# A two-layer token mixer with a mixture of experts: order of the last group's outputs, order of the first weight splits, and more expert weights on chip

## The chip, the cores and the metric

The kernel runs on one core of a Trainium2 chip. The core has a matrix engine (PE, with its weight loads shown as PEld), a vector engine (DVE), a scalar engine (ACT), a general engine (POOL) and an engine that mostly issues transfers (SP); sixteen DMA engines move data between the chip's large memory and the on-chip memory (SBUF). The metric is the device time of one execution in microseconds (us), lower is better. Before the change it is 1646.34 us, the median of three runs (1646.19 to 1651.53).

## The reference

The model has two layers on 256 tokens (`x`) and 256 context tokens (`ctx`), 1024 wide. In the last layer only the tokens go on, the context serves the mixers alone.

```
for each layer:
    mod = silu(c) @ w_mod + b_mod            # shifts, scales, gains; the same for the context
    h   = rms_norm(x) * (1 + scale) + shift
    p   = h @ w_in                           # inputs of four mixers and of their gates
    out = (sum of sigmoid(gate_i) * mixer_i(p)) @ w_mix_out     # s5, gla, window attention, conv
    x   = x + g1 * out
    x   = x + g2 * moe(rms_norm(x) * (1 + scale2) + shift2)
return rms_norm(x) * final_norm_g

moe(t):   # 4 groups of 8 experts
    the likeliest group of each token, the two best experts in it, their weights
    a = t @ w1[e];  b = t @ w3[e];  y += weight * (silu(a) * b) @ w2[e]
```

The weights of the 32 experts are 96 MB per layer, and all of them are read.

## The kernel before, in words

A planner (the tile framework) puts the instructions of each engine in order. It takes them as their data and buffers are free, earlier written ones first; instructions written under `high_priority` go ahead of all others that are ready. An explicit edge (`follow`) puts one instruction of an engine behind another. While `self.line` is a list, PE's instructions stay in the order in which they are written. Transfers of weights are all issued by SP, in one queue, in the planner's order; an issue whose buffer isn't free yet holds the queue.

**Layer start (`norm_h`, L539; `cm`, L623).** In layer 1 the two tiles of the tokens (t = 2, 3) are normed first, then those of the context (t = 0, 1): ACT squares and sums a tile, DVE makes a small value of the sum (`rnv`), POOL raises it to the power -1/2 (`rn`), and DVE (even t) or ACT (odd t) scales the tile to `xn`, which PE transposes. The first product after that, of the s5 input `u`, splits its weights into a high part (`wh`, ACT) and a low part (`wl`, DVE), in `split` under `high_priority`.

**Mix (`mix`, L1414).** Four quarters of `w_mix_out`. Each result bank is multiplied by the gain vector g1 (`prm`), which SP fetches from a scratch in the chip's memory (`vec`), and added to x. There are three result banks of this kind.

**Experts (`experts`, L1709).** The experts go in eight groups of four (`qd`). The weights of a group come in twelve quarters of 1 MB (`quarter`): j = 0 to 7 are w1 and w3 by blocks of 128 input rows, j = 8, 9 are w2's first column half, 10, 11 its second. `first` multiplies the gathered tokens by quarters 0 to 7 (`pab`), `hidden` makes silu(a) * b and transposes it, `second` multiplies by w2 (`pye`) and scales the result into `yy` (ACT the high part, DVE the low part), `combine` adds the scaled outputs into the tokens' rows with a 0/1 matrix (`pcb`), DVE multiplies by g2 (`pg`) and adds to x. The tokens of the next group are gathered by POOL (`fetch`, tile `xg`) and transposed (`pgt`).

Each group has 64 slots per expert in two blocks b of 32. In layer 0 (`PARTS` 1) both blocks serve all 512 rows. In layer 1 (`PARTS` 2, H = 2) block 0 holds slots of token tile 2 and block 1 those of tile 3.

Weights go to pools of 8 KB buffers: `wp`, used by the mixers too (three buffers in layer 0, four in layer 1), `mw` (six and nine), in layer 1 now and then the buffer of the context's x, no longer needed (`xp`, tag x0), and in layer 1 two quarters of the first group in `yy`, which later holds scaled outputs. `ahead` (L1869) names the quarters asked for before the experts start, nine and fourteen.

Tokens beyond the 64 slots of an expert are handled in a loop under a branch (`If`, L2013), not entered in these runs; in layer 0 one extra group of two experts (`x`) is computed always, beside group 6.

Of the kernel before, what the change touches and what calls it, by code (L numbers as in the profile page):

```python
# [19 lines left out]
D = 1024  # L20
# [157 lines left out]
class Net:  # L178
    def __init__(self, tc, A, out, dbg=None, stop=None):
        self.tc, self.nc, self.A, self.out = tc, tc.nc, A, out  # L180
        self.dbg, self.stop = dbg, stop
        self.line, self.behind = None, None
# [83 lines left out]
    def run(self):  # L266
        tc = self.tc
        with ExitStack() as cx:
# [11 lines left out]
            self.turns, self.spent = 0, False  # L280
# [10 lines left out]
    def consts(self):  # L291
# [9 lines left out]
        for n, sh in (("i16", [128, 16]), ("reset", [128, 512]), ("cos", [128, 256]), ("sin", [128, 256]),  # L301
                      ("rot", [128, 128]), ("mask", [128, 2, 128])):
            t = cp.tile(sh, F32, name="c_" + n)
            self.late.append((t, A[n]))
            self.cst[n] = t
# [27 lines left out]
    def slot(self, pool=None, sh=(128, 2048)):  # L333

        if pool is None:
            self.turns += 1
            if self.spent and self.turns % 4 == 0:
                return self.xp.tile(list(sh), F32, name="w", tag="x0")
        return (pool or self.wp).tile(list(sh), F32, name="w", tag="w")
# [75 lines left out]
    def vec(self, pool, l, name, s, tag="bc", **kw):  # L415

        b, q = {"g1": (0, 0), "sh2": (0, 2), "G2": (1, 0), "g2": (1, 2)}[name]
        t = pool.tile([128, D], F32, name=f"{name}{s}", tag=tag, **kw)
# [120 lines left out]
    def norm_h(self, l):  # L539

        sides = (0, 1) if l == 0 else (1, 0)
        with self.tc.tile_pool(name=f"nrm{l}", bufs=2, reuse_waits="tile") as np_:
# [15 lines left out]
            for s in sides:  # L558
                xn = []
                for t in (2 * s, 2 * s + 1):  # L560
# [8 lines left out]
                    else:  # L569
                        self.ts(xn[-1], xt, r, None, OP.mult)  # L570
# [52 lines left out]
    def cm(self, l, unit, t0, emit, blocks=(0, 1)):  # L623
# [827 lines left out]
    def moe_open(self, l):  # L1451
# [3 lines left out]
        self.spent = self.last  # L1455
# [9 lines left out]
        for n, sh in (("prio", [128, 44]), ("tok", [128, 4]), ("iota", [128, 512]), ("quad", [128, 4]),  # L1465
                      ("tri", [128, 128])):
            t = ro.tile(sh, F32, name="c_" + n)
            self.G.dma_start(t, self.A[n])
# [9 lines left out]
    def moe(self, l):  # L1478
# [6 lines left out]
        with ExitStack() as cx:  # L1485
# [3 lines left out]
            self.yy = cx.enter_context(tc.tile_pool(name=f"yy{l}", bufs=2 if self.last else 3, reuse_waits="tile"))  # L1489
            with tc.tile_pool(name=f"rl{l}", bufs=2, reuse_waits="tile") as tp:  # L1490
# [182 lines left out]
    def spread(self, pool, l, NT, R, tag):  # L1673
# [10 lines left out]
        t1 = new(NT, 32)  # L1684
# [24 lines left out]
    def experts(self, l, ep, R, more, later, hd, NT, NTOK, tiles):  # L1709
# [9 lines left out]
        g2 = {s: self.vec(ep, l, "g2", s, tag=f"g2{s}", bufs=1) for s in sorted({t // 2 for t in tiles})}  # L1719
# [148 lines left out]
        soon = [(0, 6), (0, 7)] if self.last else []  # L1868
# [266 lines left out]
```

## Time and profile before

| | |
|---|---|
| median of three runs | 1646.34 us |
| the profiled execution: its time | 1646.56 us |
| its span, first to last instruction | 1644.7 us |
| mean granted TensorE clock | 0.966 |
| PE busy | 1490.2 us, 91% |
| PEld busy | 962.2 us, 59% |
| DVE busy | 963.5 us, 59% |
| ACT busy | 534.4 us, 32% |
| POOL busy | 83.9 us, 5% |
| moved by DMA | 384.81 MB, mean 234 GB/s |

Layer 0's mix runs from about 590 to 637 us, its experts from 679 to 980; layer 1's mix from about 1331 to 1360, its experts from 1392 to 1634. A busy share is a mean over the span: what limits a stage is read from the engines and the DMA in that stage and from the waits there. A wait is put down to what came last.

### The profile page before, as it was taken

The page shows a single profiled execution, that of the slowest core. Times are in us where ns is not written, and L with a number is a line of the kernel's source. Part 1 is how long each engine was busy: PE and PEld are TensorE (multiplying, and loading weights), DVE is VectorE, ACT ScalarE, POOL GpSimd, SP SyncE. Part 2 cuts the span into 40 slices and gives each one's busy share as a digit, 9 for nine tenths or more (in the row PEclk, how much of TensorE's full clock was granted, in tenths as well). Part 3 has the DMA queues.
Part 4 walks back from the last instruction along what each step waited for, and adds up shares of the span by engine and source line. Part 5 has one row for each costly group of instructions (what it writes and reads, how often), then busy time and mean ns, then how long its engine had stood idle before and what let it go on. Part 6 is the DMA issues. An engine that isn't in the chain of part 4 may idle for free.

```text
span 1644.7 us, 26473 instructions
## 1 busy us (share of the span) xinstructions
PE 1490.2 (91%) x10595; PEld 962.2 (59%) x10595; DVE 963.5 (59%) x2252; ACT 534.4 (32%) x1044; POOL 83.9 (5%) x110
## 2 busy tenths in 40 slices
PE   4999999999998998799989989999999995998886
PEld 1566665677886797344344436686889883333221
DVE  6788998755475655544343566696676753233334
ACT  3523444342353322121111224335455431222211
POOL 0000000000000001110000000000000102000000
PEclk9899999999999999799989999999999996999998
DMA  9333254441221497899999972648624388999995
GB/s 331 141 141 131 67 191 169 151 153 52 82 98 52 139 343 271 291 386 386 384 336 392 387 270 106 215 163 294 214 78 154 101 295 288 370 384 377 379 383 213
DMA packets 147772, 384.81 MB, mean 234 GB/s; under 512 B 10167, under 2 KB 15863, under 8 KB 135612
## 3 DMA queue, kind: packets, MB, share of 16 engines
q1 hardware_dynamic: 140204, 367.65, 61.9%
q0 software_dynamic: 6864, 13.06, 2.5%
q10 hardware_dynamic: 576, 2.36, 0.5%
q8 instruction: 85, 1.39, 0.3%
q14 instruction: 43, 0.35, 0.1%
HBM read 380.81 MB, written 12.81 MB: 239 GB/s over the span
## 4 chain that ended last, share of the span: by engine, by line
PE 36%; DVE 8%; DMA 7%; issue 4%; ACT 3%; SPq 1%; POOL 1%; POOLq 0%; DVEq 0%; ACTq 0%; another core or an unknown queue 0%
PE pab L223 10%; PE pye L223 6%; PE pcm L223 6%; DMA w<-in_w_dram 4%; PE pcb L223 4%; DVE wl L201 1%; PE pbr L223 1%; PE pgt L226 1%; DVE zz L209 1%; PE pm L223 1%; PE pmix L223 1%; DMA w<-in_winc_dram 1%; ACT xT L215 1%; SPq L346 1%; PE po L223 1%
## 5 line engine op out<-in xcount | busy, mean ns | idle before, releaser
L223 PE MATMUL pcm<-hh,wh 128*128 128x512 f32 (+1 forms) x736 | 261.4, 356 | 6.0 <-ACT wh L215 3.9
L223 PE MATMUL pcm<-hl,wh 128*128 128x512 f32 (+1 forms) x736 | 259.4, 353 | 0.5 <-DVE hl L201 0.5
L223 PE MATMUL pcm<-hh,wl 128*128 128x512 f32 (+1 forms) x736 | 257.3, 350 | 1.6 <-DVE wl L201 1.6
L223 PE MATMUL pab<-w,xT 128*32 128x512 f32 x2048 | 233.7, 598 | 18.1 <-DMA w<-in_w_dram 18.1
L201 DVE TENSOR_TENSOR wl<-w,wh 128x1024 fp32r<-128x1024 f32 x128 | 155.5, 1222 | 124.2 <-ACT wh L215 119.8
L215 ACT ACTIVATE wh<-w 128x1024 fp32r<-128x1024 f32 x128 | 134.6, 1058 | 255.8 <-PE pcm L223 166.1
L223 PEld LDWEIGHTS pab<-w,xT 128*32 128x32 f32 x2048 | 62.7, 110 | 178.0 <-issue 133.3
L223 PEld LDWEIGHTS pcm<-hh,wh 128*128 128x128 f32 x736 | 140.0, 191 | 37.8 <-issue 8.3
L223 PEld LDWEIGHTS pcm<-hh,wl 128*128 128x128 f32 x736 | 139.8, 190 | 21.7 <-issue 4.4
L223 PEld LDWEIGHTS pcm<-hl,wh 128*128 128x128 f32 x736 | 139.9, 190 | 21.2 <-issue 5.3
L209 DVE SCALAR_TENSOR_TENSOR th<-th,pab 128x256 f32<-128x256 f32 (+1 forms) x33 | 13.9, 421 | 211.6 <-ACT th L212 211.6
L223 PE MATMUL pye<-w,aT 128*32 128x512 f32 x1024 | 118.8, 603 | 5.6 <-ACT xT L215 3.5
L223 PE MATMUL pcb<-yy,oT 128*128 128x512 f32 x320 | 94.9, 426 | 1.0 <-DVE pg L195 0.5
L212 ACT ACTIVATE th<-pab 128x256 f32<-128x256 f32 (+1 forms) x33 | 12.6, 383 | 253.7 <-PE pab L223 245.2
L223 PE MATMUL pm<-w,actp 128*32 128x512 f32 x384 | 68.3, 650 | 27.0 <-DMA w<-in_wmod_dram 27.0
L209 DVE SCALAR_TENSOR_TENSOR yy<-pye,ws,yy 128x512 fp32r<-128x512 f32 x64 | 48.0, 750 | 68.8 <-ACT yy L212 68.7
L195 DVE TENSOR_TENSOR pg<-g,pcb 128x512 f32<-128x512 f32 x96 | 64.8, 684 | 37.5 <-PE pcb L223 35.9
L223 PEld LDWEIGHTS pcb<-yy,oT 128*128 128x128 f32 x320 | 57.0, 194 | 44.9 <-issue 19.1
L223 PE MATMUL ptk<-wl,hh 128*128 128x256 f32 x288 | 82.5, 287 | 0.0
L223 PE MATMUL ptk<-wh,hl 128*128 128x256 f32 x288 | 82.2, 285 | 0.0
L223 PE MATMUL ptk<-wh,hh 128*128 128x256 f32 x288 | 82.1, 285 | 0.0
L212 ACT ACTIVATE yy<-pye,ws 128x512 fp32r<-128x512 f32 x64 | 44.0, 687 | 104.8 <-PE pye L223 104.8
(408 smaller groups left out, 2527.2 us busy)
## 6 DMA issues: line engine op xcount, KB each, us to landing
w<-in_w_dram SPq DMA_DIRECT2D x198, 1024.0 KB
w<-in_wmod_dram SPq DMA_DIRECT2D x48, 1024.0 KB
w<-in_winc_dram SPq DMA_DIRECT2D x42, 1024.0 KB
w<-in_wint_dram SPq DMA_DIRECT2D x10, 1024.0 KB
w<-in_wout_dram SPq DMA_DIRECT2D x10, 1024.0 KB
w<-in_wmix_dram SPq DMA_DIRECT2D x8, 1024.0 KB
dtb<-T SPq DMA_DIRECT2D x4, 1472.0 KB
T<-dtb SPq DMA_DIRECT2D x4, 1472.0 KB
```

What stands on the lines that cost most here:

```text
L195: return self.V.tensor_tensor(o, a, b, op=OP.mult)
L201: return self.V.tensor_tensor(o, a, b, op=OP.subtract)
L209: return self.V.scalar_tensor_tensor(o, a, s, b, op0=op0, op1=op1)
L212: return self.S.activation(o, a, f, bias=bias, scale=scale, **k)
L215: return self.S.activation(o, a, AF.Copy, bias=0.0, scale=1.0)
L223: return self.queue(self.T.matmul(o, l, r, start=start, stop=stop, **k))
L226: return self.queue(self.T.transpose(o, a, ident))
L346: (eng or self.Y).dma_start(v, src)
```

## The change

1. **Splits.** In layer 1 the low-part splits of the first product are ordered on DVE behind the scaling of tile 2 (`self.normed`).
2. **One room for constants.** The constants `reset`, `cos`, `sin`, `rot`, `mask` and `i16` share one tile, `i16` now last. In layer 1 the room is used again: its first 1024 columns for the g2 vector, the next for 256 columns of `iota` (512 before) and for `tri`.
3. **Buffers.** A new pool `mx1` with one buffer in layer 0 and two in layer 1. Loads go through a fixed list of homes in turn: layer 0 six of `mw`, one of `mx1`, three of `wp`; layer 1 the x0 buffer, nine of `mw`, four of `wp`, two of `mx1`. `ahead` is as long as the list. Mix weights no longer use x0.
4. **yy.** Quarters 5, 6 and 7 of the first group in layer 0 (6 and 7 in layer 1) go to `yy`. All but quarter 7 are asked for ahead of the second norm; quarter 7 behind the branch, in the buffer that the branch's body uses for its outputs (`yyx`).
5. **Last group of layer 1.** `second` takes the block as the outer loop, block 1 first, and the column half as the inner one. `combine` sorts by side (t // 2) first, then by half.

```diff
-    def split(self, src, hi, lo):
+    def split(self, src, hi, lo, last=None):
         self.copy(hi, src)
-        self.sub(lo, src, hi.bitcast(F32))
+        i = self.sub(lo, src, hi.bitcast(F32))
+        if last is not None:
+            self.follow(i, last)
...
-                        self.ts(xn[-1], xt, r, None, OP.mult)
+                        i = self.ts(xn[-1], xt, r, None, OP.mult)
+                        self.normed = i if l > 0 and s == sides[0] else None if l == 0 else self.normed
...
-                self.split(w[:, i], wh, wl)
+                self.split(w[:, i], wh, wl, self.normed)
+            if i == len(blocks) - 1:
+                self.normed = None
...
+            self.mx1 = cx.enter_context(tc.tile_pool(name=f"mx{l}", bufs=2 if self.last else 1, reuse_waits="tile"))
+            self.soon = [self.weight(self.A["w13"][l][0:4, 1, :, j].rearrange("e p f -> p e f"), self.yy)
+                         for j in ((2,) if self.last else (1, 2))]
...
+        if self.last:
+            homes = [self.xp] + [self.mw] * 9 + [None] * 4 + [self.mx1] * 2
+        else:
+            homes = [self.mw] * 6 + [self.mx1] + [None] * 3
         def load(src):
             seq[0] += 1
-            return self.weight(src, None if seq[0] % (7 if self.last else 3) in ((0, 3) if self.last else (0,)) else self.mw)
+            return self.weight(src, homes[(seq[0] - 1) % len(homes)])
...
-        soon = [(0, 6), (0, 7)] if self.last else []
-        ahead = [(qd, j) for qd in range(2) for j in range(12) if (qd, j) not in soon][:14 if self.last else 9]
+        soon = [(0, 6), (0, 7)] if self.last else [(0, 5), (0, 6), (0, 7)]
+        ahead = [(qd, j) for qd in range(2) for j in range(12) if (qd, j) not in soon][:len(homes)]
...
-        for k in soon:
-            ready[k] = self.weight(quarter(*k), self.yy)
+        for k, w in zip(soon, self.soon):
+            ready[k] = w
+        yyx = self.yy.tile([128, 2, 2, 512], F32R, name="yyx", tag="w")
...   (behind the branch)
+        for _ in soon[:-1]:
+            self.slot(self.yy)
+        ready[soon[-1]] = self.weight(quarter(*soon[-1]), self.yy)
...   (second)
-            for hf in range(2):
-                for b in range(g["nb"]):
+            if qd == nq - 1 and H == 2:
+                order = [(hf, b) for b in (1, 0) for hf in range(2)]
+            else:
+                order = [(hf, b) for hf in range(2) for b in range(g["nb"])]
+            for hf, b in order:
...   (combine)
-            for hf in range(2):
-                for i, t in sorted(enumerate(tiles), key=lambda p: -(p[1] // 2)):
+            order = [(hf, i, t) for hf in range(2) for i, t in enumerate(tiles)]
+            order.sort(key=lambda p: (-(p[2] // 2), p[0]) if nq - 1 in qds and H == 2 else (p[0], -(p[2] // 2)))
+            for hf, i, t in order:
```

The last group's steps are driven as before: two outputs, one output, two sums, one output, the other two sums.

## Rows read from the trace of the kernel before

**Rows 1.** The page's head: the span.
```profile
span 1644.7 us, 26473 instructions
```
**Rows 2.** Stretches: length, busy us (instructions) by engine, PE's clock, DMA share, GB/s.
```profile
573.00:606.00 33.00, 33.00 (x209) 30.00 (x208) 16.26 (x26) 10.02 (x12) 0.00 (x0) 1.00 0.92 329
1344.00:1380.00 36.00, 21.30 (x147) 19.32 (x147) 21.47 (x64) 7.77 (x15) 5.10 (x6) 0.77 1.04 390
1380.00:1396.00 16.00, 8.79 (x50) 5.07 (x54) 3.69 (x24) 2.39 (x4) 4.10 (x4) 0.56 0.47 153
1396.00:1620.00 224.00, 199.79 (x1662) 68.37 (x1654) 76.50 (x174) 46.86 (x87) 11.87 (x12) 1.00 1.04 377
```
**Rows 3.** Chain of waits: start, us, what. First products of three groups.
```profile
679.35 14.53 PE pab L223 x128
...
1419.69 13.73 PE pab L223 x128
1446.69 3.41 PE pab L223 x29
```
**Rows 4.** PE's waits: total us, times, longest. First 775 to 845, then from 1392.
```profile
PE pgt L226 <- DMA xgx<-h2d,atx: 7.8, 1, 7.8
PE pab L223 <- DMA w<-in_w_dram: 2.6, 4, 0.8
...
PE pab L223 <- DMA w<-in_w_dram: 15.4, 21, 0.8
```
**Rows 5.** Timeline of the end: start, length, engine, what, idle before and releaser.
```profile
1627.43 1.06 PE L223 MATMUL pye<-w,aT 128*32 128x512 f32 x8 [1.60 <-DMA w<-in_w_dram]
1628.42 1.20 PE L223 MATMUL pcb<-yy,oT 128*128 128x512 f32 x4
1629.55 1.92 PE L223 MATMUL pye<-w,aT 128*32 128x512 f32 x16
1631.41 1.38 PE L223 MATMUL pcb<-yy,oT 128*128 128x512 f32 x3
1631.54 0.69 ACT L212 ACTIVATE yy<-pye,ws 128x512 fp32r<-128x512 f32 x1 [2.30 <-PE pye L223]
1632.38 0.75 DVE L209 SCALAR_TENSOR_TENSOR yy<-pye,ws,yy 128x512 fp32r<-128x512 f32 x1
1633.18 0.50 PE L223 MATMUL pcb<-yy,oT 128*128 128x512 f32 x1 [0.40 <-DVE yy L209]
```
**Rows 6.** Transfers issued, 1320 to 1394 us, then 580 to 679 us.
```profile
w<-in_w_dram SPq DMA_DIRECT2D x16, 1024.0 KB
...
w<-in_w_dram SPq DMA_DIRECT2D x9, 1024.0 KB
```
**Rows 7.** Timeline of SP's queue, 1384 to 1385 us.
```profile
1384.77 0.38 SPq L346 DMA_DIRECT2D w<-in_w_dram  x1
```
**Rows 8.** The gather xg: issue to landing; 1375 to 1400, then 1400 to 1600.
```profile
DMA to landing us min/median/max: 4.2/4.5/6.6
...
DMA to landing us min/median/max: 6.3/6.9/7.4
```
**Rows 9.** Timeline: a mix weight's fetch; g1, its first product, a weight split.
```profile
999.51 0.37 SPq L346 DMA_DIRECT2D w<-in_wmix_dram  x1
...
595.98 1.38 SPq L421 DMA_DIRECT2D g<-dmod  x2
606.50 0.76 DVE L209 SCALAR_TENSOR_TENSOR prm<-pmix,g 128x256 f32<-128x256 f32 x2 [2.08 <-DMA g<-dmod]
610.48 1.06 ACT L215 ACTIVATE wh<-w 128x1024 fp32r<-128x1024 f32 x1 [7.32 <-PE pmix L223]
```
**Rows 10.** Timeline of layer 1's start on DVE and ACT.
```profile
980.56 2.36 DVE L201 TENSOR_TENSOR wl<-w,wh 128x1024 fp32r<-128x1024 f32 x2
982.84 0.15 DVE L206 TENSOR_SCALAR rnv<-ss 128x1 f32<-128x1 f32 x1
984.35 0.21 DVE L206 TENSOR_SCALAR rnv<-ss 128x1 f32<-128x1 f32 x2
985.16 1.15 ACT L212 ACTIVATE xn<-x,rn 128x1024 f32<-128x1024 f32 x1 [0.99 <-POOL rn L353]
```

More of the change, by code (lines that the diff above doesn't have):

```diff
@@ L300, in consts @@
         self.late = []
[L301 to L303 removed]
+        self.room = cp.tile([128, 1424], F32, name="room")
+        at = 0
+        for n, w in (("reset", 512), ("cos", 256), ("sin", 256), ("rot", 128), ("mask", 256), ("i16", 16)):
+            t = self.room[:, at:at + w]
+            at += w
+            if n == "mask":
+                t = t.rearrange("p (a b) -> p a b", a=2)
             self.late.append((t, A[n]))
@@ L333, in slot @@
     def slot(self, pool=None, sh=(128, 2048)):
[L335 to L339, printed above, removed]
+        return (pool or self.wp).tile(list(sh), F32, name="w", tag="x0" if pool is not None and pool is self.xp else "w")
     def weight(self, src, pool=None, eng=None):
@@ L417, in vec @@
         b, q = {"g1": (0, 0), "sh2": (0, 2), "G2": (1, 0), "g2": (1, 2)}[name]
-        t = pool.tile([128, D], F32, name=f"{name}{s}", tag=tag, **kw)
+        t = self.room[:, 0:D] if pool is None else pool.tile([128, D], F32, name=f"{name}{s}", tag=tag, **kw)
         src = self.dmod[l][b]
@@ L1466, in moe_open @@
                       ("tri", [128, 128])):
-            t = ro.tile(sh, F32, name="c_" + n)
-            self.G.dma_start(t, self.A[n])
+            if self.last and n == "iota":
+                t = self.room[:, 1024:1280]
+                self.G.dma_start(t, self.A[n][:, 0:256])
+            elif self.last and n == "tri":
+                t = self.room[:, 1280:1408]
+                self.G.dma_start(t, self.A[n])
+            else:
+                t = ro.tile(sh, F32, name="c_" + n)
+                self.G.dma_start(t, self.A[n])
             self.cst[n] = t
@@ L1683, in spread @@
         H = PARTS[l]
-        t1 = new(NT, 32)
+        t1 = (new(NT, 32) if tag == "sm" else
+              pool.tile([128, 256], F32, name="th")[:, 0:NT * 32].rearrange("p (t e) -> p t e", t=NT))
         base = new(H, 32)
@@ new lines, in combine @@
+                todo = []
+                for qd in qds:
+                    g = gb[qd]
+                    for b in range(g["nb"]):
+                        s = spans[b] if g["nb"] == 2 else slice(0, NTOK)
+                        if s.start <= i * 128 < s.stop:
+                            todo += [(g["oT"][b][:, i * 128 - s.start:(i + 1) * 128 - s.start], g["y"][hf, b][:, p])
+                                     for p in range(2)]
+                pc = self.mx(name="pcb")
+                for j, (o, y) in enumerate(todo):
+                    self.mm(pc, o, y, j == 0, j == len(todo) - 1)
@@ L1984, in go @@
+                pg = ep.tile([128, 512], F32, name="pg", tag="pg")
+                self.mul(pg, g2[t // 2][:, cols], pc)
+                xv = self.x[t // 2][:, t % 2, cols]
+                self.add(xv, xv, pg)
+                yield
         def go(steps, n=None):
@@ L2010, in experts @@
         most = max((min(2, m) * NTOK - m * (SL - 31)) // 32 for m in range(1, NEXP + 1))
-        lent = [(0, j) for j in range(3 * MORE)]
+        lent = ahead[:3 * MORE]
         v = self.nc.values_load(R["num"][0:1, 0:1], min_val=0, max_val=most)
@@ L2022, in experts @@
                 go(extra(r))
+                gb["x"]["yt"] = yyx
                 first("x")
```

58 lines of the change are left out of this document (22 added, 36 removed).

## Prediction

> **What bounds the kernel now.** I read the page first, then the chain of waits, the engines' busy time by stretch, and the waits of PE, of the DMA queue and of the tiles that the change names. The page shows PE busy for nine tenths of a span of 1644.7 us [rows 1], which hides that the two expert stages have different limits.
>
> In layer 1's expert stage the DMA is the limit. From 1396 to 1620 us its share is 1.04 at 377 GB/s [rows 2]. PE needs 27.0 us for a group of four experts when its weights are there (1419.69 to 1446.69) [rows 3], but twelve loads of 1.05 MB take 33.4 us at 377 GB/s, so the weights fall behind: PE waits 21 times for a load in that stage, 15.4 us in all [rows 4], and the last quarter lands only when the last outputs want it, at 1627.43 [rows 5]. What moves that landing is how much is on chip before the first experts begin. Between 1380 and 1396 us the DMA moves only 153 GB/s, against 390 just before [rows 2]: 16 x (390 - 153) = 3.8 MB of room, 9.7 us, left empty because every buffer is full and waits for PE.
>
> In layer 0's expert stage PE is the limit. Of the waits between 775 and 845 us only 2.6 us are for weights; 7.8 us are for the extra group's gather, which the change leaves as it is [rows 4].
>
> **The change part by part.** The sum is made against the profiled execution's own 1646.56 us (span 1644.7 and 1.9 around it); it lies 0.2 above the median of 1646.34.
>
> *More loads, layer 1.* The new list has 1 + 9 + 4 + 2 = 16 homes, plus two quarters in the yy pool: 18 quarters before the first expert matmul has freed a buffer. The trace of before counts 16, not 14 [rows 6]: fifteen ahead of the branch and one behind it at 1384.77, into a buffer that the old rule left over [rows 7]. So the gain is two loads, not four. At 390 GB/s a load is 2.7 us, and the room of 9.7 us holds both: -5.4 us at the end of the stage. Against it stands the first gather, which now meets a busy DMA. Around this empty stretch a gather lands 4.2 to 6.6 us after issue, in the full stage 6.3 to 7.4, median 6.9 [rows 8]. The second half's gather decides when PE starts, and it is the slow one of the four (6.6), so I add 1.1 us, between 0 and 2.9 (7.4 less 4.5). PE's start sets the first free buffers, so this comes off the gain: **-4.3**, from -5.4 to -2.5. The g2 vector moves to the shared room and can be fetched earlier, but this only widens the empty stretch: nothing. A mix weight and the first expert quarter change places between the x0 buffer and the ring, one load each way: nothing.
>
> *More loads, layer 0.* Nine loads before the first expert [rows 6] become 10 in homes and 3 in yy. PE waited 2.6 us for weights between 775 and 845 and, by the same rows, its next wait is the gather; four loads more are 10.9 us of lead, so these waits go: **-2.6**, from -2.6 to 0. What is late next is PE itself, so the rest of the lead buys nothing.
>
> *What the early loads push.* The first two yy buffers of layer 0 lie, by adding up the pools, on the room of the s5 pool, which is free once layer 0 has copied its last table out, before the mix; and the planner fetches a weight as soon as its buffer is free, as the mix weight fetched at 999.51, long before layer 1's mix, shows [rows 9]. These loads then go ahead of the gain vector g1 in SP's queue, at a time when the DMA is 0.92 busy. g1 was issued at 595.98 and its first product waited for it until 606.50 and ended at 607.26, which frees the result bank that PE wants next. The split of the next weights waited for PE to be through the first half of the current ones, until 610.48 [rows 9]: so late only because PE took up the freed bank when it came. There is no cover left, so each us that g1 is late is a us of PE. The bounds are 0 (loads behind g1, or in gaps) and 5.4 (both loads fully ahead). The share of 0.92 over 33 us leaves 2.6 us of gaps, so 2.8 is left if the loads are ahead; as their place in the queue is open, I take about half, **+1.5**.
>
> A rule of the Trainium skill speaks against the change here: DMA: Bandwidth & Descriptors, section Two DMAs through the same engine are not ordered, says that within one queue of one DMA engine descriptors start in order, so a small vector issued on SP stands behind each weight issued before it. The 10.5 us from g1's issue to its use agree with it. By that rule this term is the full 5.4 and the time 1649.5; it is a rival below.
>
> *Last group's order.* Outputs were made by column half, first half for both token blocks, then the second. Now they go by token block, block 1 first. The sums are sorted by minus t//2, but in layer 1 the tiles are 2 and 3, both with t//2 = 1, so their order stays: first half of tile 2 (block 0), of tile 3 (block 1), then the second halves. So each pair of sums begins with the block whose outputs have just been issued. PE takes its work in written order, and after the last weights' landing it does, before: half an output, four matmuls of sums, an output, four of sums, from 1627.43 to 1633.68, 6.25 us with one wait of 0.40 [rows 5]. After: the second half of (half 1, block 1) 1.06, output (0,0) 1.92, then a wait for its scaling (from the output's end at 1631.47 over ACT's 0.69 and DVE's 0.75 to PE's start at 1633.18 is 1.71), four of sums 1.20, output (1,0) 1.92, again 1.71, and 1.20: 10.72 us. **+4.5**. Nothing covers it: it lies behind the last landing, and the final norm waits for the last sum. Below, two round trips less the wait that goes, 2 x 1.71 - 0.40 = 3.0, if the weights were earlier than PE; so 3.0 to 4.5.
>
> *First splits behind the norm.* Two splits (wl) hold DVE for 2.36 us from 980.56, and the first tile's scale chain starts behind them at 982.84 [rows 10]. They now follow the first tile's scaling. But the second tile's chain begins with its own small DVE operation, which before came right behind that scaling (984.35); the splits have high priority and their inputs are ready, so they land between the two, and ACT's scaling of the second tile, which the transposes need (985.16), starts when it did. First tile 2.2 earlier, second unmoved: **+0.2**, from -2.2 (if the planner puts the second tile's operation ahead) to +0.3.
>
> *The rest.* The constants in one tile load in another order (i16 last), half of iota is loaded in layer 1, and a scratch tile is shared inside the branch's body: each lies beside other work, nothing.
>
> Sum: -4.3 - 2.6 + 1.5 + 4.5 + 0.2 = **-0.7**, so 1645.9 for a profiled execution and **1645.6** against the median. With all ends on one side: -5.4 - 2.6 + 0 + 3.0 - 2.2 = -7.2, and -2.5 + 0 + 5.4 + 4.5 + 0.3 = +7.7; the likeliest case's own range is 1639 to 1654.
>
> **Rivals.**
> - *The change does what it says* (0.20). Four more loads count in layer 1 too and fill the whole room of 9.7 us, the norm chain gains 2.2, g1 is not pushed: 1646.3 - 9.7 - 2.6 - 2.2 + 4.5 = 1636.3; and 1631.8 if the new order costs nothing. For it: the room is there in the trace. Against it: before had 16 loads out, and both reorderings, read in the code, lead elsewhere.
> - *g1 behind both loads* (0.16): 1649.5, by the order in SP's queue, as above. Against it: two small gaps in that stretch.
> - *The last quarter of the first half comes too late* (0.13), on the slower side. In both layers quarter 7 is now loaded behind the branch, in a buffer that passes through two stand-in tiles. If its load waits until PE has read quarters 5 or 6, it starts at about 679.35 + 7 x 1.82 = 692.1 in layer 0 [rows 3], where PE wants it, and lands behind the five loads that PE's first reads have released by then, an estimate of 5 x 2.7 = 13.5 us. Layer 0 is bound by PE, so this adds 13.5: 1659.1. In layer 1 the loads queued behind keep the DMA busy and nothing is added. It decides as soon as the load lands after 692.1. Against it: in layer 1 the first load behind the branch went out at 1384.77, ahead of PE's first expert matmul [rows 7].
> - *Forecast* (0.51): 1645.6.
>
> **How the numbers follow.** A measurement of this kernel can tell about 0.5% (8.2 us) from no change, so faster means under 1638.1 and slower over 1654.6. Faster 0.20 is the first rival; slower 0.13 the third; same 0.67 the forecast and the second. The range of 1635 to 1655 takes in the first rival's nearer part and the ends of the unknown costs, and leaves out the third.
>
> **What would show it.** In the profile after: 18 loads of experts before layer 1's first expert matmul, and the DMA's empty stretch before it shorter by some 5 us; the last load landing some 4 us earlier relative to that start, and two waits of about 1.7 us of the last sums for the scaled outputs, with 10.7 us from the landing to the last sum; no waits of PE for weights in layer 0's third and fourth groups; the two splits between the two tiles' scale chains at layer 1's start; g1's product after 607 by the clock of the mix stage. It would be wrong if PE waits for quarter 7, if the last sums follow their outputs without a wait, or if PE stalls long in layer 0's mix.

## The result, and the profile after: slower by 0.67%

The changed kernel takes 1658.22 us (median of five runs, 1654.97 to 1661.63); the kernel before took 1650.32 beside it on the same chip (1646.19 to 1651.53). The ratio is 1.0067 [1.005, 1.0083], compared round by round, so it need not be the quotient of the medians. 1645.6 with a range of 1635 to 1655 had been forecast, and a chance of 0.13 for slower. The forecast stood on 1646.34 us for the kernel before; that times the ratio is 1657.4, still above the range. The direction was wrong and the range too low.

The profiled execution took 1654.97 us, 8.41 above that of before; its span grew by 8.47 [rows 1]:

```profile
span 1653.2 us, 26493 instructions
```

Times between the same instructions of the two traces, after less before, put this difference in its stretches. Forecast are the terms of the prediction's sum:

| stretch | us | forecast |
|---|---|---|
| start to the end of layer 0's mixers | +2.15 | 0 |
| layer 0: mix | -0.04 | +1.5 |
| layer 0: route, and from it to the first expert matmul | +2.01, +1.43 | 0 |
| layer 0: experts | -1.87 | -2.6 |
| layer 1: last sums of layer 0 to norm's last transposes | +1.0 | +0.2 |
| layer 1: mixers, mix, route | -0.3 | 0 |
| layer 1: end of route to the first expert matmul | +4.90 | +1.1 |
| layer 1: first to last expert matmul | -4.59 | -5.4 |
| last expert matmul to the end | +3.8 | +4.5 |

In the first row the change touches only how the constants are loaded, and kernels that are alike up to there differ by more: in the three kernels of this document with the code of before there, layer 0's mixers end at 590.5, 593.4 and 596.8 us. So this row is put down to the spread between executions.

*Layer 1's start of the experts.* PE's waits from 1390 to 1402 us in the profile after (total us, times, longest):

```profile
PE pgt L228 <- DMA xg<-h2d,at: 8.6, 1, 8.6
PE pab L225 <- SPq L2046: 3.8, 1, 3.8
```

The second row is new. L2046 is the branch's `If` (L2013 before), and SPq the queue of the engine that issues the weights. That queue's own waits, 1340 to 1405 us:

```profile
SPq L2046 <- SPq L2046: 12.8, 2, 12.4
SPq L349 <- PE pmix L225: 12.2, 1, 12.2
```

Before had there, in layer 1:

```profile
SPq L2013 <- SPq L2013: 0.5, 1, 0.5
```

The issues in the profile after (start, length, queue, line, what, count), and PE's first steps behind them:

```profile
1344.42 8.09 SPq L349 DMA_DIRECT2D w<-in_w_dram  x2
...
1364.67 21.86 SPq L349 DMA_DIRECT2D w<-in_w_dram  x10
...
1401.61 0.38 SPq L349 DMA_DIRECT2D w<-in_w_dram  x1
```

```profile
1393.93 3.56 PE L228 MATMUL pgt<-ident,xg 128*128 128x128 f32 x16 [8.59 <-DMA xg<-h2d,at]
...
1401.27 1.93 PE L225 MATMUL pab<-w,xT 128*32 128x512 f32 x8 [3.77 <-SPq L2046]
```

The tokens are transposed at 1397.5, and PE stands until 1401.27 for SP, which stands in the branch for 12.4 us. Only then does the eighteenth load go out, 0.34 us behind PE's first expert matmul. Seventeen went out ahead of the branch (one at 1004.54, the others from 1336.32 on). What SP waits for stands in the trace's records of semaphores, the counters through which engines and transfers report to each other. At the end of the branch SP has nine short instructions that wait for a semaphore:

```profile
L2046 SPq EVENT_SEMAPHORE  x9: 17/17/17, 1388.2 to 1401.1; - x9
```

The last eight of them wait for the semaphores through which SP's loads report that they have landed. The last of the seventeen loads landed at 1400.60 and the wait for it ended at 1400.63. The stretches show the same (length, PE, PEld, DVE, ACT, POOL busy, granted clock, DMA share, GB/s):

```profile
1380.00:1396.00 16.00, 3.46 (x17) 2.98 (x18) 7.83 (x51) 0.89 (x3) 2.12 (x2) 0.50 1.05 388
1396.00:1404.00 8.00, 4.23 (x24) 2.06 (x27) 0.00 (x0) 1.70 (x3) 1.98 (x2) 0.72 0.52 167
1404.00:1630.00 226.00, 204.91 (x1704) 70.67 (x1694) 76.51 (x174) 47.87 (x89) 11.87 (x12) 0.99 1.02 372
```

The hole of before (153 GB/s from 1380 to 1396, [rows 2]) is full, as forecast; a new one stands behind it, where the loads run out while SP stands in the branch and issues nothing.

*The end.* Timeline from the last landing, to be read against [rows 5]:

```profile
1632.09 2.78 PE L225 MATMUL pye<-w,aT 128*32 128x512 f32 x24 [1.59 <-DMA w<-in_w_dram]
1635.68 0.51 PE L225 MATMUL pcb<-yy,oT 128*128 128x512 f32 x1 [0.81 <-ACT yy L212]
1636.46 0.97 PE L225 MATMUL pcb<-yy,oT 128*128 128x512 f32 x3 [0.28 <-DVE yy L209]
1637.36 1.93 PE L225 MATMUL pye<-w,aT 128*32 128x512 f32 x16
1640.27 0.51 PE L225 MATMUL pcb<-yy,oT 128*128 128x512 f32 x1 [0.98 <-ACT yy L212]
1641.06 0.97 PE L225 MATMUL pcb<-yy,oT 128*128 128x512 f32 x3 [0.28 <-DVE ms L206]
```

One and a half outputs, a wait, sums, an output, a wait, sums: 9.94 us to 1642.03, where before took 6.25.

*Layer 0.* PE's waits from 781 to 851 us no longer name expert weights [rows 4]; the gather alone is left long:

```profile
PE pgt L228 <- DMA xgx<-h2d,atx: 9.3, 1, 9.3
```

g1's product came at its usual place in the mix, 1.9 us later by the clock [rows 9], after a start that was 2.15 later. The early loads were issued behind g1, ahead of the next layer's modulation weights:

```profile
608.43 0.76 DVE L209 SCALAR_TENSOR_TENSOR prm<-pmix,g 128x256 f32<-128x256 f32 x2 [1.86 <-DMA g<-dmod]
```

```profile
630.27 8.82 SPq L349 DMA_DIRECT2D w<-in_w_dram  x2
639.87 19.82 SPq L349 DMA_DIRECT2D w<-in_wmod_dram  x5
```

*Layer 1's norm*, against [rows 10]:

```profile
983.18 1.06 ACT L215 ACTIVATE wh<-w 128x1024 fp32r<-128x1024 f32 x1 [6.87 <-DVE pg L195]
984.15 1.04 ACT L215 ACTIVATE wh<-w 128x1024 fp32r<-128x1024 f32 x1
985.09 1.04 ACT L212 ACTIVATE xn<-x 128x1024 f32<-128x1024 f32 x1
986.26 0.15 DVE L206 TENSOR_SCALAR rnv<-ss 128x1 f32<-128x1 f32 x1 [1.90 <-ACT xn L212]
987.10 0.76 DVE L205 TENSOR_SCALAR xn<-x,rn 128x1024 f32<-128x1024 f32 x1 [0.69 <-POOL rn L356]
987.77 2.36 DVE L201 TENSOR_TENSOR wl<-w,wh 128x1024 fp32r<-128x1024 f32 x2
990.04 0.21 DVE L206 TENSOR_SCALAR rnv<-ss 128x1 f32<-128x1 f32 x2
```

The splits (wl) stand between the two tiles' chains, as forecast. But the first tile gained next to nothing, since ACT's two copies (wh) stand ahead of its first square at 985.09. They begin 0.84 us behind the end of layer 0's last sum; before they began 1.23 us ahead of it.

### The profile page after: what moved, and what is told of

It is laid out like the page before. It is cut to its first block, busy times and chain, and to the rows that moved or that the text cites. A ratio compares the mean times of both kernels' runs of the same rounds, so it can differ in the third digit from the quotient of the medians.

```text
span 1653.2 us, 26493 instructions
## 1 busy us (share of the span) xinstructions
PE 1487.0 (90%) x10595; PEld 966.4 (58%) x10595; DVE 962.0 (58%) x2252; ACT 533.7 (32%) x1044; POOL 83.5 (5%) x110
## 5 line engine op out<-in xcount | busy, mean ns | idle before, releaser
L225 PEld LDWEIGHTS pcm<-hl,wh 128*128 128x128 f32 x736 | 140.9, 191 | 20.8 <-issue 4.7
L225 PE MATMUL pm<-w,actp 128*32 128x512 f32 x384 | 64.1, 648 | 27.9 <-DVE a L201 19.0
L225 PEld LDWEIGHTS pye<-w,aT 128*32 128x32 f32 x1024 | 30.3, 111 | 75.8 <-issue 60.6
```

The source lines that it names most:

```text
L225: return self.queue(self.T.matmul(o, l, r, start=start, stop=stop, **k))
```

## The experiments

Each kernel is the changed one with an edit, except the two named before_. Stretches in us, from each profile: A0 layer 0's mix to the end of route; B0 from there to the first expert matmul; C0 first to last expert matmul; N1 layer 0's last sum to layer 1's last transposes of the norm; B1, C1 as B0, C0 in layer 1; E last expert matmul to the end. Each row is one execution; the ratio is that of 6 to 12 executions in other rounds (5 for the change).

| kernel | A0 | B0 | C0 | N1 | B1 | C1 | E | ratio to before |
|---|---|---|---|---|---|---|---|---|
| before | 33.7 | 8.9 | 280.3 | 19.1 | 11.0 | 226.6 | 26.1 | 1 |
| the change | 35.7 | 10.3 | 278.4 | 20.1 | 15.9 | 222.0 | 29.9 | 1.0067 [1.005, 1.0083] |
| tail_before | 37.2 | 10.2 | 276.8 | 20.9 | 15.6 | 221.9 | 26.0 | 1.0026 [1.0009, 1.0043] |
| tail_by_block | 36.8 | 10.2 | 276.8 | 20.8 | 16.9 | 222.6 | 27.7 | 1.0035 [1.0019, 1.0051] |
| soon_late_1 | 36.9 | 10.4 | 277.4 | 21.0 | 12.2 | 221.5 | 31.3 | 1.0025 [1.0011, 1.0039] |
| soon_late_0 | 36.7 | 10.4 | 279.1 | 21.0 | 16.1 | 223.2 | 32.5 | 1.0046 [1.0028, 1.0063] |
| l0_back | 33.5 | 8.6 | 280.3 | 21.0 | 14.9 | 222.1 | 29.9 | 1.0053 [1.0035, 1.007] |
| behind_0 | 36.0 | 7.9 | 279.1 | 21.2 | 16.0 | 223.6 | 32.5 | 1.0067 [1.0041, 1.0094] |
| behind_1 | 36.1 | 10.4 | 278.7 | 21.0 | 10.0 | 224.9 | 31.4 | 1.0038 [1.0023, 1.0054] |
| norm_back | 36.3 | 10.0 | 277.4 | 19.5 | 15.9 | 223.2 | 32.5 | 1.0055 [1.0035, 1.0076] |
| before_tail | 32.7 | 8.6 | 279.1 | 19.1 | 9.8 | 227.1 | 32.1 | 1.0038 [1.0022, 1.0053] |
| before_norm | 34.3 | 9.3 | 279.1 | 20.7 | 11.8 | 227.4 | 26.1 | 1.001 [0.9994, 1.0027] |
| best_nine | 33.5 | 8.4 | 280.0 | 21.1 | 11.1 | 224.1 | 26.0 | 1.0018 [1.0005, 1.0032] |
| best_three | 33.6 | 8.1 | 278.5 | 21.1 | 10.6 | 224.4 | 26.0 | 0.9987 [0.9973, 1.0001] |
| best_norm_out | 33.8 | 9.8 | 277.4 | 19.5 | 10.0 | 224.2 | 26.0 | 0.9976 [0.9961, 0.9991] |
| best_norm_act | 33.9 | 8.2 | 278.7 | 20.8 | 10.7 | 224.1 | 26.0 | 0.9976 [0.9963, 0.9989] |

**The last group's order.** tail_before gives outputs and sums the order of before; tail_by_block keeps the new outputs and sorts the sums so that they want the block whose outputs came first.

```diff
-            if qd == nq - 1 and H == 2:
+            if False:                              # tail_before
...
-            order.sort(key=lambda p: (-(p[2] // 2), p[0]) if nq - 1 in qds and H == 2 else (p[0], -(p[2] // 2)))
+            order.sort(key=lambda p: (p[0], -(p[2] // 2)))       # tail_before
...
-            (-(p[2] // 2), p[0]) if nq - 1 in qds and H == 2
+            (-p[1], p[0]) if nq - 1 in qds and H == 2            # tail_by_block, in the same key
```

> The changed kernel with the last group's outputs and sums in the order of before; nothing else is undone. In the changed kernel the last sum ends 9.94 us behind the last landing (1632.09 to 1642.03), before 6.25. Theory A (the order costs what the trace shows): 6.2 to 6.4 us again, the time 3.7 us shorter than the changed kernel's. Theory B (the landing alone sets the end, and the last sums follow it within a fixed time): 9 to 10 us still, no change. Everything ahead of the last group is that of the changed kernel, so mix and route of layer 1 should again show the branch's stall (first expert matmul about 15.9 us behind the last small matmul of the route; before 11.0) if that stall belongs to the change and not to one execution.

> The changed kernel, with the last sums sorted by token block (block 1 first), as its outputs are, in place of t//2, which is 1 for both tiles. Theory A (only the sums' order fails: they wait for outputs just issued): the last sum ends 6.3 us behind the last landing, as before. Theory B (the outputs' order by itself puts one output more behind the landing, 1.92 us): by the rows of the changed kernel two waits go, one at the end stays, so about 8.1 us (9.94 less 1.8). Theory C (sums wait for nothing that an order can change): 9.9.

From the last landing to the last sum tail_before took 6.85 us, near the 6.25 of before. tail_by_block took 8.56, the 8.1 of an order that itself puts one more output behind the landing:

```profile
1631.06 2.78 PE L225 MATMUL pye<-w,aT 128*32 128x512 f32 x24 [1.58 <-DMA w<-in_w_dram]
1633.77 1.21 PE L225 MATMUL pcb<-yy,oT 128*128 128x512 f32 x4
1634.91 1.92 PE L225 MATMUL pye<-w,aT 128*32 128x512 f32 x16
1636.77 0.73 PE L225 MATMUL pcb<-yy,oT 128*128 128x512 f32 x2
1637.89 0.49 PE L225 MATMUL pcb<-yy,oT 128*128 128x512 f32 x1 [0.40 <-ACT yy L212]
1639.13 0.49 PE L225 MATMUL pcb<-yy,oT 128*128 128x512 f32 x1 [0.75 <-DVE yy L209]
```

Its first sums follow their outputs without a wait. Of the 3.7 us that the change adds here, some 2 belong to the outputs' order and the rest to the sums' key. In time, the interval of tail_before lies below the change's.

before_tail is the kernel before with nothing but the new order of outputs; in layer 1 the sums go as before by either key.

```diff
+            order = [(hf, b) for b in (1, 0) for hf in range(2)] if qd == nq - 1 and H == 2 else \
+                    [(hf, b) for hf in range(2) for b in range(g["nb"])]
+            for hf, b in order:
```

> The kernel before, with the changed order of the last group alone. From the last expert matmul to the end it is 26.1 us before, 26.0 and 27.7 in the two kernels that undo or mend the order, and 29.9 to 32.5 in the seven that have it. Theory A (the order alone costs this): 29.9 to 32.5, the time 4 to 6 us longer than before, of which up to 2.6 with TensorE's granted clock at half in this stretch, as six of the seven have it. Theory B (the clock falls there because the stage ahead of it ends otherwise): 29.9 with a full clock. Everything ahead of it as before: layer 0's mix end to last expert matmul 322.9, layer 1's last sum of layer 0 to end of its branches 352.3, route to last expert matmul 237.6, each within 1 us if one profile is enough to tell.

It is slower, and its end longer by 5.9 us, more than the change's 3.8. The difference is the granted clock: in the profile after, half clock lies ahead of the last landing, here it covers the landing and what follows it. Stretches of the end of before_tail (columns as above):

```profile
1616.42:1619.70 3.28, 1.66 (x12) 0.56 (x12) 1.29 (x4) 1.15 (x3) 0.00 (x0) 1.00 1.04 388
1619.70:1629.94 10.24, 8.77 (x44) 1.40 (x40) 1.50 (x2) 1.37 (x2) 0.00 (x0) 0.50 0.22 82
1629.94:1637.31 7.37, 5.18 (x28) 1.76 (x24) 4.47 (x8) 2.59 (x6) 0.00 (x0) 1.00 0.00 0
```

Half clock (0.50, the level of 1.2 GHz) for 10.24 us. 24 matmuls of outputs took 5.09 us there, as the timeline shows, against 2.78 in the profile after:

```profile
1625.24 5.09 PE L223 MATMUL pye<-w,aT 128*32 128x512 f32 x24 [0.74 <-DMA w<-in_w_dram]
```

Eight of the sixteen kernels give layer 1's last group the change's order of outputs and sums; their end is 29.9 to 32.5 us, and seven of the eight show half clock for 3.4 to 10.2 us in that stretch (for 3.4 in the profile after, ahead of the last landing). The other eight, tail_by_block among them, show none there. PE had been waiting before the fall (busy 1.66 of 3.28 us above). Why the clock falls with this order is not settled.

**Layer 1's loads.** soon_late_1 asks for the early quarter in `yy` behind the other sixteen loads; behind_1 asks for fourteen ahead of the branch, and for four behind it.

```diff
-                         for j in ((2,) if self.last else (1, 2))]
+                         for j in ((2,) if self.last else (1, 2))] if not self.last else []      # soon_late_1
...   (behind the loads of ahead)
-        for k, w in zip(soon, self.soon):
-            ready[k] = w
+        for i, k in enumerate(soon[:-1]):
+            ready[k] = self.soon[i] if self.soon else self.weight(quarter(*k), self.yy)
...
+        held = ahead[len(ahead) - 2:]               # behind_1
+        ahead = ahead[:len(ahead) - 2]
...   (behind the branch)
+        for k in soon:
+            ready[k] = self.weight(quarter(*k), self.yy)
+        for k in held:
+            ready[k] = load(quarter(*k))
```

> The changed kernel; in layer 1 the one expert load that stood ahead of the norm (quarter 6, yy buffer) is issued behind the 16 others. Theory A (that load waits on SP for a buffer under the mix stage, 1349.07 to 1364.67, and nine loads with free buffers stand behind it): the hole in SP's issues goes, the DMA moves some 385 GB/s from 1350 to 1380 by that clock (now 332 and 290), the loads land 7 to 9 us earlier, the branch's join, which waits for them, passes at about 1392 in place of 1401.1, and the first expert matmul is released by the gather, 3.8 us earlier; the end of the stage follows by 3 to 5 us. Theory B (the hole is filled by bytes that have to be moved anyway): join and first expert matmul within 1 us of the changed kernel's.

> The changed kernel; in layer 1 fourteen loads ahead of the branch and four right behind it, in place of seventeen and one. Theory A (the branch's join waits on SP for every load issued ahead of it, and the first expert matmul for the join; the loads need not stand ahead of it): the join passes some 8 us earlier, the first expert matmul comes 11 to 12.2 us behind the route's last matmul, released by the gather (with seventeen: 15.6 to 16.9), and the stage from it to the last expert matmul stays at 222, because the four loads fill the time until PE frees buffers: 4 us shorter. Theory B (four loads behind the join come too late to fill it): first expert matmul 11 to 12.2 but the stage 226 as before, no gain. Theory C (the join waits for something else than those loads): 15.6 to 16.9 still.

In soon_late_1 SP's wait of 12.2 us that the mix's matmuls (pmix) ended is gone: the early quarter's buffer, not free until then, had held the queue with the other loads behind it. The branch still waits, but ends sooner:

```profile
SPq L2046 <- SPq L2046: 7.6, 2, 7.2
```

```profile
1364.00:1380.00 16.00, 9.64 (x67) 7.99 (x65) 7.08 (x13) 4.95 (x10) 5.04 (x6) 0.69 1.04 393
1392.00:1400.00 8.00, 4.04 (x20) 3.25 (x24) 0.00 (x0) 1.99 (x4) 0.99 (x1) 0.50 0.35 121
```

The first expert matmul now follows the gather and its transposes without a gap:

```profile
1395.96 3.80 PE L228 MATMUL pgt<-ident,xg 128*128 128x128 f32 x16 [8.50 <-DMA xg<-h2d,at]
1399.69 3.24 PE L225 MATMUL pab<-w,xT 128*32 128x512 f32 x24
```

B1 falls from 15.9 to 12.2, and the stage keeps its gain (221.5). The last of the loads ahead of the branch landed 31.3 us behind the mix's end, against 35.8 with the change: some 4.5 us earlier, not the 7 to 9 that were expected. In time, the interval of soon_late_1 lies below the change's too. In behind_1 the wait is gone altogether:

```profile
SPq L2048 <- SPq L2048: 0.5, 1, 0.5
```

```profile
1390.33 8.79 SPq L349 DMA_DIRECT2D w<-in_w_dram  x5
```

```profile
1388.00:1392.00 4.00, 0.35 (x2) 0.38 (x3) 1.57 (x10) 0.00 (x0) 1.30 (x2) 0.50 0.45 117
1392.00:1400.00 8.00, 7.28 (x48) 3.88 (x50) 0.00 (x0) 2.39 (x4) 1.98 (x2) 0.66 1.02 371
```

PE starts 10.0 us behind the route, sooner than before, and pays with a stage of 224.9, since the DMA is idle ahead of the branch's end again. B1 and C1 together are 234.9, against 237.6 before, 237.9 with the change and 233.7 in soon_late_1: 2.7 and 3.9 us of the lead are kept. In time the intervals of behind_1 and of the change overlap a little. The three kernels show what the branch's end does: SP leaves when the loads that it issued ahead have landed (12.4 us, and 7.2 with an earlier start); with none in flight, at once (0.5). The other traces bear it out. The sixteen kernels pass the branch 32 times, once in each layer. In 25 passages a load was still out when SP came to wait for it, and each time its wait ended 0.03 us behind the last landing (soon_late_1: 1397.49 and 1397.52). In the other seven, all in layer 1 of kernels that issue fewer loads ahead of the branch, the nine instructions took 0.6 to 0.8 us.

**Layer 0's loads.** l0_back has the nine loads of before and none early; soon_late_0 asks for the early two behind the other ten; behind_0 asks for four of the thirteen behind the branch.

```diff
-            homes = [self.mw] * 6 + [self.mx1] + [None] * 3
+            homes = [self.mw, self.mw, None] * 3                   # l0_back, soon = []
+            homes = [self.mw] * 6 + [None] * 3 + [self.mx1]        # behind_0, the last behind the branch
...   (soon_late_0: as soon_late_1, with the test turned round)
+                         for j in ((2,) if self.last else (1, 2))] if self.last else []
```

> The changed kernel with layer 0's loads as before: nine expert loads ahead of the branch and none early in the yy buffers; layer 1 untouched. Theory A (the four added loads, wherever they stand ahead of the branch, slow layer 0's route and gather: mix end to first expert matmul is 46.0 to 47.4 us in the four kernels with them, 42.6 before): 42.6 to 43.5, and the expert stage loses its gain (first to last expert matmul 280.3, with them 276.8 to 279.1). Net 1 to 2 us shorter than the changed kernel's. Theory B (the route is slower through another part of the change: constants in one tile, the planner's order): 46 or more still, and 280.3 for the experts, so 2 us longer.

> The changed kernel; in layer 0 the two expert loads that stood ahead of the norm (yy buffers) are issued behind the ten others instead. In the changed kernel the first expert matmul comes 46.0 us behind the mix stage's end (638.81 to 684.83), before 42.6 us. Theory A (the early loads push the next layer's modulation weights, whose matmuls PE then does between the router's): back to 42.6 to 44. Theory B (the added bytes themselves slow the gather and hold the branch's join, wherever they stand): 46 or more. Theory C (chance of one execution): the two other kernels of this batch, which are untouched there, spread as widely as this one differs.

> The changed kernel; in layer 0 the same nine loads ahead of the branch as before, and the four added ones issued right behind it. Theory A (what costs is that they stand ahead of the branch, not that they are loaded): mix end to first expert matmul 42.6 to 43.5 as before, and the expert stage keeps 277 to 278.5; 3 to 4 us shorter than the changed kernel's. Theory B (quarter 5 is then too late): a wait of some us of the first group's expert matmuls for a load, stage 281 or more. Theory C (the route is slow for another reason): 46 still.

With nine loads A0 + B0 is 42.1, as before (42.6), and C0 280.3; with the change it is 46.0 and 278.4. So the four loads gain 1.9 in the stage and cost 3.4 ahead of it. Issuing the early two later (47.1) returns nothing. behind_0 did not come out as meant: the planner put the load into `mx1` ahead of the branch, before the modulation weights (637.86), A0 stayed at 36.0, while B0 fell to 7.9. PE's order of the next layer's modulation (`pm`) and of the router's matmuls (`plg`) is that of before in the kernels with nine loads ahead of the branch, whose A0 is 32.7 to 34.3, and another in the rest; load and order came together in every run, so which of them costs the 2 to 3.5 us stays open. PE's wait for the modulation weights is not it: 4.5 us from 660 to 695 with the change, 4.9 in l0_back. Nor is it the branch: SP stands there for 10.4 us in layer 0 with the change (6.5 before), but of the sixteen kernels only norm_back has PE's first expert matmul of layer 0 wait for it, 0.8 us. In time none of the three can be told from the change.

**The norm's order.** norm_back is the change without it, before_norm the kernel before with it alone.

```diff
-                self.split(w[:, i], wh, wl, self.normed)
+                self.split(w[:, i], wh, wl)         # norm_back; before_norm: the other way round
```

> The changed kernel without the order that puts layer 1's first weight splits behind the first tile's scaling. From layer 0's last sum to the last transposes of layer 1's norm it is 20.1 to 21.0 us in the five kernels with that order, 19.15 before. Theory A (the splits land between the two tiles' scale chains and hold up the second): 19.1 to 19.4, and 1 to 1.6 us shorter to layer 1's branches. Theory B (it is the plan around it that differs): 20 to 21 still. Theory C (the order helps the input products behind the norm, which then start with weights ready): 19.2, but given back by the next 40 us.

> The kernel before, with layer 1's first weight splits ordered behind the first tile's scaling, and nothing else. Theory A (the splits hold up the second tile): from layer 0's last sum to the norm's last transposes 20.1 to 21 us (before 19.15, and 19.46 in the changed kernel without the order), and from layer 0's last sum to the end of layer 1's branches 353.5 to 355 (before 352.3). Theory B (the next stage gives it back): 20.1 to 21, but 352.3 to the branches' end. My sum had +0.2.

N1 is 19.1 to 19.5 in the four kernels without the order and 20.1 to 21.2 in the others: it costs some 1.6 us there. Where, the first transposes of the first tile show (in brackets the idle time since layer 0's last sum), in the kernel before, in before_norm and in the changed one:

```profile
984.49 1.11 PE L226 MATMUL pth<-ident,xn 128*128 128x128 f32 x4 [5.85 <-DVE rnv L206]
...
988.35 1.11 PE L228 MATMUL pth<-ident,xn 128*128 128x128 f32 x4 [3.58 <-DVE xn L205]
...
987.91 1.12 PE L228 MATMUL pth<-ident,xn 128*128 128x128 f32 x4 [5.57 <-DVE xn L205]
```

In before_norm the first tile comes 2.27 us earlier and the second 0.4 later (9.04 us behind the sum, before 8.63), much as forecast; the 1.6 us are lost on the context's two tiles, whose transposes end last. In the changed kernel the first tile gains 0.28 and the second comes at 10.62, because ACT's copies come later. Those copies begin 1.2 to 1.5 us ahead of the last sum's end in the seven kernels with nine loads ahead of layer 0's branch and these copies unordered, and 0.84 or 0.85 behind it in the eight with more. l0_back, which differs from the changed kernel in layer 0's loads alone, has them early and its first transposes at 3.58. So this part hangs on layer 0's loads and not on the order. How the loads move the copies is not shown. To the end of layer 1's mixers the 1.6 us cannot be followed: from layer 0's last sum 352.3 us before, 355.6 in before_norm, 354.4 in norm_back, 354.6 with the change, with 6.8 to 17.1 us at half clock in each. Both ratios leave it open.

**Versions put together.** best_three takes the order of before at the end, behind_1, and in layer 0 nine loads ahead of the branch and three in `yy` behind it; best_nine has nine alone in layer 0. best_norm_out is best_three without the norm's order. best_norm_act puts ACT's copies behind the second tile's square and the low parts behind its small operation.

```diff
-        self.copy(hi, src)
+        j = self.copy(hi, src)
...
+            self.follow(j, last[0])                 # best_norm_act: the second tile's square on ACT
+            self.follow(i, last[1])                 # its rnv on DVE
```

> The changed kernel with the last group's order of before; layer 0 loads nine quarters ahead of the branch and three right behind it, layer 1 fourteen ahead and four behind. Theory A (each loss of the change has its own place, and what it gains does not need those places): mix end to first expert matmul in layer 0 42.1 to 43 us, first to last expert matmul 277.5 to 279 (before 280.3), layer 1 from the route's last matmul to the last expert matmul 234 to 235.5 (before 237.6), and from there to the end 26 (before 26.1): 4 to 5 us shorter than before, less what layer 1's norm gives away. Theory B (the planner's order differs for other reasons and the loads only move waits): layer 0 at 46 again or layer 1 at 237 to 239, and no gain over before.

> As the kernel with three loads behind layer 0's branch, but with layer 0's nine loads alone, as before. Theory A (the early loads' only use in layer 0 is against PE's waits for weights in its third and fourth groups): layer 0 from mix end to last expert matmul 322 to 323, as before, 1.5 to 2.5 us longer than with the three; the rest as there. Theory B (three loads behind the branch gain nothing): the same in both, within 0.5.

> The kernel with three loads behind layer 0's branch and before's last group, now also without the order that puts layer 1's first splits behind the first tile's scaling. Theory A (that order costs 1.6 us at the norm and nothing gives it back): from layer 0's last sum to the norm's last transposes 19.1 to 19.5 us (with it 21.07), to the end of layer 1's branches 352 to 353 with a full clock there, 354 to 354.5 with one dip of 3.4 us (with the order 353.8 to 354.1 without a dip, 355 to 356 with one); all else as in that kernel, so 1.5 to 2 us shorter: 0.997 to 0.9985 of the kernel before. Theory B (given back): branches' end 354 without a dip, time as with it.

> The same kernel, with both halves of the first splits ordered: ACT's copies (wh, 2.0 us for two) behind the second tile's square, DVE's differences (wl, 2.4 us for two) behind the second tile's first small operation. Theory A (the order of the change fails twice: ACT's copies still stand ahead of the first square, 983.18 to 985.19 in the changed kernel, and DVE's differences stand ahead of the second tile): with both out of the way the norm's last transposes come 17 to 17.6 us behind layer 0's last sum (before 19.15), and the branches' end 350 to 351.5 without a clock dip; 1.5 to 2.5 us shorter than without any order. Theory B (the input products behind the norm then wait for the late splits): 17 to 17.6, but 352 to 353 to the branches' end.

best_norm_out takes 1644.69 us against 1649.4 and best_norm_act 1646.05 against the same: ratios of 0.9976 both, the intervals under 1: a quarter of a per cent under the kernel before and, going by the two ratios, some 0.9% under the changed one. best_three comes out better than best_nine by 1.5 us from layer 0's mix to its last expert matmul (320.3 against 321.8), and the intervals of the two ratios just miss each other: three loads behind the branch help a little in layer 0. In best_norm_act the first transposes came 3.58 us behind the last sum, as in before_norm, and the second tile's 7.28 us behind it (8.63 before). But the norm as a whole did not get shorter (20.8): the last tile, of the context, was squared on ACT 10.6 us behind the last sum, 7.6 before. POOL's power for the second tile ran beside DVE's low parts, which had begun 0.16 us earlier, and took 1.47 us (the other two 0.57 and 0.55):

```profile
981.35 0.57 POOL L357 TENSOR_TENSOR rn<-rnv,mhalf 128x1 f32<-128x1 f32 x1 [96.23 <-DVE rnv L206]
982.86 1.47 POOL L357 TENSOR_TENSOR rn<-rnv,mhalf 128x1 f32<-128x1 f32 x1 [0.93 <-DVE rnv L206]
986.87 0.55 POOL L357 TENSOR_TENSOR rn<-rnv,mhalf 128x1 f32<-128x1 f32 x1 [2.55 <-DVE rnv L206]
```

The Trainium skill, SBUF — State Buffer, section Who interferes with whom, says that a DVE instruction with both inputs in SBUF contends with a GpSimd instruction that reads SBUF, and that the order of issue decides which of the two blocks. The 0.9 us of POOL, here the later one, agree with it.

## Why the prediction was wrong

- *More loads, layer 1 (-4.3, measured +0.3)*: **the step that failed.** Its pieces came out: lead in the stage -4.6 (forecast -5.4), slower gather +1.06 (+1.1), two loads more. What the step left out is the branch between the loads and the experts, whose price it put at nothing without a reason. The runs put in its place: SP leaves the branch when the loads that it issued ahead have landed, and PE's first expert matmul (3.8 us) and SP's next issue (12.4 us) wait for SP. Before, the wait was 0.5 us because the last load had landed at 1383.83, just as SP came to the branch's end (1383.71): the step counted as free room the hole that begins there. The sign stood in the trace of before, in layer 0 from 665 to 690 us, where loads are in flight at the branch, and was not read:

```profile
SPq L2013 <- SPq L2013: 6.5, 3, 3.6
```

- A second cause lies in the same step. The early quarter was costed as a load that goes out when its buffer is free. It is taken into the queue in the planner's order and stood there from 1352.5 to 1364.67 with nine loads behind it; in soon_late_1, where it stands behind them, the next load went out at 1354.65. soon_late_1 gives 3.7 us of B1 back for it.
- *More loads, layer 0 (-2.6)*: right in kind, -1.9; the waits for weights went. *What the early loads push (+1.5)*: wrong place. They were issued behind g1, the mix kept its length, and the rival with 5.4 us did not occur; so what loads ahead of g1 would cost was not put to the test. The cost, +3.4, came in the route and the gather, for which the sum had nothing; whether by the loads themselves or by PE's order is open.
- *Last group's order (+4.5)*: right mechanism, +3.8 in the profile. The waits for the scaled outputs are 0.81 + 0.28 and 0.98 + 0.28, not 1.71, as the first of the four sums needs ACT's part alone. Over the eight kernels with the order the end is 29.9 to 32.5, 3.8 to 6.4 over before, the upper values with half clock, which no term held.
- *First splits (+0.2)*: +1.0 in the profile, some 1.6 over all kernels. The order on DVE came as forecast. By itself it also moved the two tiles as forecast (before_norm: 2.27 earlier, 0.4 later), but the step left out the context's tiles behind them, which come later. In the changed kernel ACT's copies, later than before, took the first tile's gain as well.
- *Rivals*: quarter 7 was never waited for. That the change does what it says failed on the branch, on the count of loads (two more, not four) and on the norm, which did not gain its 2.2.

By stretch the sum misses 4.6 in layer 1's loads, 2.6 in layer 0's, -0.7 at the end and 0.8 in the norm, 7.3 of 9.2 us. The remaining 1.9 are the start of layer 0 (2.15) less 0.3 in layer 1's mixers, mix and route. Without the start, which is chance, the time would still have risen where a fall was forecast.

## What to carry to other kernels

In this kernel a prefetch across a branch was free only while it landed before SP came to the branch: look in the profile for waits of the issuing queue on the branch's own line, in any layer, before filling an idle DMA ahead of it, and issue the rest behind the branch. A load whose buffer comes free late belongs behind the others in an in-order queue. When the order of products is changed, the order of their consumers must be read with its actual tile numbers.

## What the runs showed of the hardware that had not been expected

- At a branch's end the issuing engine waited until the loads that it had issued ahead had landed; the wait ended 0.03 us behind the last landing in 25 passages of 25 with a load still out. Seventeen loads of 1 MB ahead of it made this 12.4 us (7.2 with the early load moved back, 0.5 with none in flight), and another engine's first matmul behind the branch 3.8 us late.
- PE was granted half clock in the last group's stretch in seven of eight kernels with the change's order there and in none of eight without, for as much as 10.24 us; the ends of the seven differ by 2.6 us (29.9 to 32.5).
- A POOL operation on 128 values took 0.9 us longer beside DVE's subtraction of two tiles in SBUF (1.47 us). In the trace of before the same operation took 1.54 and 1.46 us in layer 0, beside DVE's additions to `h`, and 0.57 or 0.55 alone.
